# One core, layer 0 and 1 of a diffusion backbone: the body recorded first, then issued in the order of a list schedule of single instructions

## The chip, the cores and the metric

One core of a Trainium2 chip runs the whole program in one launch. The metric is the device time of that launch in microseconds (us); the median over runs is given. Engines are named as in the profile: PE multiplies matrices and PEld loads its weights, DVE, ACT and POOL work on vectors, SP issues nearly all DMAs. Results of PE land in PSUM, which has eight banks, each holding a tile of 128 x 512 fp32.

## What is computed

512 latent tokens and 256 context tokens of width 1024 pass through two layers; the output is the latent stream after a last RMS norm. Layer 0 mixes tokens by windowed attention and by a bidirectional RWKV-7 recurrence, layer 1 by a Fourier transform; each layer then has a squared-ReLU MLP of width 4096. Shift, scale and gate of every norm come from products of a conditioning row with ada_w.

```python
for i in range(DEPTH):
    mod = (s_lat @ ada_w[i] + ada_b[i])[:, None, :]
    sh1, sc1, gt1, sh2, sc2, gt2 = jnp.split(mod, N_MOD, axis=-1)
    h = modulate(rmsnorm(x, norm1_g[i]), sh1, sc1)
    ...
    if even:
        y, yc = hybrid_ab_mixer(h, hc, mix_w_in[j], mix_w_out[j], ...)
    else:
        y = fourier_mixer(h, fourier_w_out[j])
    x = x + gt1 * y
    x = x + gt2 * channel_mlp(modulate(rmsnorm(x, norm2_g[i]), sh2, sc2), mlp_w1[i], mlp_w2[i])
return rmsnorm(x, final_g)
```

The recurrence, per head, token by token, once forward and once backward:

```python
s_kk = jnp.einsum('bhvk,bhk->bhv', S, kk_t)
S = S * w_t[:, :, None, :] - s_kk[..., None] * (kk_t * a_t)[:, :, None, :] + v_t[..., None] * k_t[:, :, None, :]
y_t = jnp.einsum('bhvk,bhk->bhv', S, r_t)
```

## The kernel before

**Precision and weights.** Activations and weights of the dense parts are split into a high and a low half (`fp32r`), and each product is three matmuls: `mm3` (L306 to L308). A weight tile comes by a load of 128 x 512 on SP's queue (`loadh`, L283, from a ring of five buffers `st`), ACT casts its high half (`whi`, L294), DVE subtracts the low half (`wlo`, L295).

**Stages in time.** First adaA (the modulation of the first norm), x and context are loaded, PE turns adaA into shift and scale (`arow`, L441 to L445), and the first three of twenty projection tiles are computed together, latent half (`lat`) then context half (`con`). Tiles 3 to 19 follow (`inproj`): eight `mm3` of 128 x 512 for the latent tokens, eight of 128 x 256 for the context where a tile has one. A tile's end (`post`) shifts it along the tokens (`shifted`, ACT and DVE, L555 to L559), builds keys, values, decay and rates (`key`, `vproj`, `lora` at L633 to L635), and spills them to DRAM (`spill`). From these pages (`page`) each of six blocks of 128 tokens builds its chunk matrices (`prep`, `chunkmats`, `naturals`, `inverse`). The recurrence is a chain over chunks of 64 tokens: `chain_u`, `chain_s`, `chain_y`, where each chunk needs the state of the one before. Attention (`attn0` to `attn2`) runs between them, then the output projection (`outA`, `read`, `outhalf`), MLP 0, the Fourier mixing, MLP 1 and the last norm.

**The other ada products.** 80 columns of adaB (`ada_bg`, L377 to L395) are computed beside the rest: for the first 24, which have two loads each, POOL multiplies (L388) and ACT sums (L389); for the other 56, in MLP 0, DVE does both in one instruction (L391), out of the same ring `st` as the weights.

**What sets the order.** `body` calls the framework directly, inside a Tile context, whose own scheduler places the instructions of each engine. The order of calls in the mixer is a string, PLAN (L1316), in which `:2000` behind a piece is a priority offset; `after(key)` keeps some instructions behind a named one (`tc.issue_after`). Each PSUM tag has banks of its own, three for `mm`, two for `rk`, two for `ch` and one for `iv`, and `phase` names the stage, by which `pst` writes one or two dummy matmuls into a newly taken bank of the attention scores, the reads and the chunk matrices (WARM, L223).

```python
WARM = {('attn1', 'mm'): 1, ('read', 'rk'): 2, ('EB', 'rk'): 1}
PSB = {"mm": 3, "rk": 2, "ch": 2, "iv": 1}
```

Of the kernel before, what the change touches and what calls it, by code (L numbers as in the profile page):

```python
# [5 lines left out]
F32 = mybir.dt.float32  # L6
# [195 lines left out]

def body(tc, I, out):
    nc = tc.nc
# [10 lines left out]
    WARM = {('attn1', 'mm'): 1, ('read', 'rk'): 2, ('EB', 'rk'): 1}  # L215
    PH = [""]
    PSB = {"mm": 3, "rk": 2, "ch": 2, "iv": 1}

    def pst(tag, shape=(128, 512), name="ps"):
        p = ps.tile(list(shape), F32, tag=tag, bufs=PSB[tag], name=name)  # L220
        for _ in range(WARM.get((PH[0], tag), 0)):
            a = p[:]
            pe.matmul(bass.AP(tensor=a.tensor, offset=a.offset, ap=[a.ap[0], [1, 512]]), identr, identr.unsqueeze(1).to_broadcast([128, 4, 128]), start=True, stop=True)  # L223
        return p
# [15 lines left out]
    act.copy(identr, ident)  # L240

# [68 lines left out]
    NI = {}  # L310

    def after(key):
        return tc.issue_after(NI[key].ins) if key else ExitStack()

    def norm_rows(pool_, xs, n, tag, pg="E", pt="E", eng=None, bcast=True):
# [17 lines left out]
        for i in range(nt):  # L333
            for j, a in enumerate(acc):
                NI["p1"] = pe.matmul(p1[:, i : i + 1], a[:, 128 * i : 128 * i + 128], ones1, start=j == 0, stop=j == len(acc) - 1)
# [7 lines left out]
        for i in range(nt):  # L343
            NI["p2"] = pe.matmul(p2[:, 128 * i : 128 * i + 128], rs[:, i : i + 1].to_broadcast([128, 128]), ident, start=True, stop=True)
# [10 lines left out]

    def phase(name):
        PH[0] = name.rstrip("0123456789") if not name.startswith("attn") else name
# [75 lines left out]
    phase("ada0")  # L433
# [100 lines left out]
    def inproj(m, ctx=True):  # L534
        if m < GRP:
            return gl_[m], gctx(m)
        phase(f'proj{m}')
        w = split_w(load(I["win"][m]))
        pl = pst("mm")
        for k in range(8):  # L540
            with after(("lora", m - LT, k) if ("lora", m - LT, k) in NI else None):
                mm3(pl, w, k, hx[k], k == 0, k == 7)
        pc = None
        if ctx:
            pc = pst("ch" if m < 14 else "mm")
            for k in range(8):
                mm3(pc[:, :C], w, k, hc[k], k == 0, k == 7)
        return pl, pc

    def shifted(m, z, pl, pc=None):  # L550
# [3 lines left out]
        for p, off, n in (((pc, 0, C),) if ctx else ()) + ((pl, C if ctx else 0, T),):  # L554
            NI["sh"] = act.activation(z[:, off : off + n], p[:, :n], AF.Identity, scale=mc)  # L555
# [17 lines left out]
    def key(hp, pl, pc):  # L573
        phase(f"key{hp}")
# [27 lines left out]
    def lowrank(pl, pc):  # L602
        phase("lowrank")
# [11 lines left out]
    def lora(hp):  # L615

        phase(f"lora{hp}")
# [9 lines left out]
        for a in range(2):  # L627
            for d in range(2):
                cols = slice(128 * d, 128 * d + 128)
                th = p4((128, TC), "th")  # L630
                for lat, o, n in ((0, 0, C), (1, C, T)):
                    p = pst("rk")
                    pe.matmul(p[:, :n], L_[:, a, cols], x1(a, lat), start=True, stop=False)  # L633
                    NI["lora", hp, 4 * a + 2 * d + lat] = pe.matmul(p[:, :n], hi[:, a, cols], X2[lat], start=False, stop=True)
# [21 lines left out]
    def prep(i, d):  # L656

        phase(f"prep{i}")
# [63 lines left out]
    def chunkmats(i, j):  # L722

        phase(f"EB{i}")
# [31 lines left out]
    def naturals(i, j):  # L756

        phase(f"nat{i}")
# [20 lines left out]
    def inverse(i):  # L779
        phase(f"inv{i}")  # L780
# [116 lines left out]
    def chain_u(i, j):  # L897

        phase(f"chain{i}")
# [29 lines left out]
    def chain_s(i, j):  # L929

        phase(f"chain{i}")
# [16 lines left out]
    def chain_y(i, j):  # L948

        phase(f"chain{i}")  # L950
# [23 lines left out]
    def vproj(hp, pl, pc):  # L974
        phase(f"vproj{hp}")
# [10 lines left out]
    def rproj(hp, pl):  # L986
        phase("rproj")
# [28 lines left out]
    def attk(pl, pc):  # L1016
        phase("attk")
# [7 lines left out]
    def attv(pl, pc):  # L1025
        phase("attv")
# [6 lines left out]
    def attkv():  # L1033

        phase("attkv")
# [31 lines left out]
    def qproj(j, pl):  # L1067
        phase("attq")
# [8 lines left out]
    def gproj(pl):  # L1077
        phase("gate")
# [13 lines left out]
    def attn0(b):  # L1092

        phase("attn1")
# [16 lines left out]
    def attn1(b, kv):  # L1111

        phase("attn1")
# [18 lines left out]
    def attnm(b):  # L1132

        phase("attn1")
# [21 lines left out]
    def attn2(b):  # L1156

        phase("attn2")
# [49 lines left out]
    def bonus(w):  # L1208
        phase("bonus")
# [25 lines left out]
    def outA(ms):  # L1235
        phase("outprojA")
# [12 lines left out]
    def read(w):  # L1249

        phase("read")
# [40 lines left out]
    LT = 2  # L1292
# [14 lines left out]
    def do_ada(n):  # L1307
        with after("sh" if "sh" in NI else None):
            ada_bg(n)
# [7 lines left out]
    tile 0, tile 1, post 0, lora 0, tile 2, post 1, lora 1, tile 3, post 2, lora 2, tile 4, post 3, lora 3, tile 5:300,  # L1317
    ada 2, post 4, prep 0 0:2000, ada 4, prep 0 1, tile 6, post 5, mats 0 0, mats 0 1:2000, nat 0 0:2000, nat 0 1:2000,
    inv 0, tile 7, ada 6, post 6, tile 8, ada 8, post 7, ada 10, tile 9, tile 10, ada 12, post 8:2000, post 9, tile 11,
    ada 14, post 10:500, tile 12, ada 16, post 11, rope, tile 14:200, post 12:1000, prep 1 0:1000, prep 1 1:200,  # L1320
    mats 1 0:200, mats 1 1:200, nat 1 0, nat 1 1:1000, tile 15, post 14, inv 1:300, tile 16, ada 18, post 15,
    prep 2 0:2000, prep 2 1:2000, mats 2 0:2000, mats 2 1:2000, nat 2 0:2000, tile 17, ada 20, post 16, tile 18, ada 22,
    tile 19, post 17, inv 2:1000, post 18:300, ada 24:300, nat 2 1:500, tile 13, post 19, post 13, kv, u 0 0, s 0 0,
    u 0 1, s 0 1, prep 3 0:500, prep 3 1:500, u 1 0:300, s 1 0:300, mats 3 0:500, mats 3 1:1500, nat 3 0:1500,
    nat 3 1:1500, inv 3:1500, qry 0:2000, max 0 0:2000, u 1 1:300, max 0 1:200, row 0:200, s 1 1:300, prep 4 0:1000,
    bonus 2:1000, prep 4 1:1000, mats 4 0:1000, mats 4 1:1000, nat 4 0:1000, nat 4 1:1000, inv 4:1000, ed 2 0,
    ed 2 1:1000, u 2 0, s 2 0, y 2 0, u 2 1, s 2 1, y 2 1, prep 5 0, prep 5 1, mats 5 0, mats 5 1, nat 5 0, inv 5,
    attn 0, bonus 3, ed 3 0, ed 3 1:300, u 3 0, s 3 0:1000, y 3 0:1000, u 3 1:1000, s 3 1:1000, y 3 1:2000, qry 1:200,
    max 1 0:200, max 1 1, row 1:200, u 4 0:100, s 4 0:100, ed 4 0, ed 4 1:100, y 4 0, bonus 4:200, u 4 1, attn 1:1500,
    qry 3:1500, max 3 0:1000, ed 5 1:1500, y 4 1, s 4 1, u 5 0:200, s 5 0:300, ed 5 0, max 3 1:500, row 3:500,  # L1330
    bonus 5:500, y 5 0, u 5 1, y 5 1, attn 3:200, qry 2:500, max 2 0:200, max 2 1:200, row 2:200, attn 2:200, out 0:200,
    out 1, out 2:200, out 3:200, out 4:200, out 5:200, out 6:700, out 7:700, read 4:700, read 5, read 3:300, read 2:300
    """
    for piece in PLAN.replace("\n", " ").split(","):
        what, _, ahead = piece.strip().partition(":")
        what, *args = what.split()
        with tc.high_priority(offset=int(ahead)) if ahead else ExitStack():
            WORK[what](*map(int, args))
    ada_bg(24)
    phase("outproj")  # L1340
# [58 lines left out]
    IA = (None, "p1", "p2")  # L1399
    IB = 2  # L1400

    def mlp(l, xs, ai, sh, gt, nxt):

        phase(f'mlp{l}norm')
# [5 lines left out]
        for f in range(NG):  # L1410
# [7 lines left out]
            with after(IA[f]):  # L1418
                for k in range(8):
                    mm3(p, w, k, us[k], k == 0, k == 7)  # L1420
# [13 lines left out]
        phase(f'mlp{l}')  # L1434
# [92 lines left out]
    phase('fourier')  # L1527
# [7 lines left out]
    for gp in range(2):  # L1535
        for t in range(4):
            p = pst(("mm", "mm", "mm", "ch", "ch", "iv", "mm", "mm")[4 * gp + t], (128, 2, 256))
            with after("p1" if 4 * gp + t >= IB else None):
                for gi in range(2):
                    g = 2 * gp + gi  # L1540
                    for k in range(2):
                        hi, lo = hs[2 * g + k]
                        sl = slice(128 * t, 128 * t + 128)
                        ch, cl = cshi[:, 256 * k : 256 * k + 256], cslo[:, 256 * k : 256 * k + 256]
                        pe.matmul(p[:, gi, :], hi[:, sl], ch, start=k == 0, stop=False)
                        pe.matmul(p[:, gi, :], hi[:, sl], cl, start=False, stop=False)
# [156 lines left out]
```

## Time and profile before

| | |
|---|---|
| runs (us) | 1482.78, 1480.8, 1479.2 |
| median (us) | 1480.8 |
| the profiled execution (us) | 1480.75 |
| its span in the profile (us) | 1479.0 |
| mean granted PE clock | 0.959 |
| dummy matmuls (L223) | 132 |

In the rows below, times are in us from the start of the span. Busy times of a stretch are the time in which an engine worked on an instruction; a PE clock of 1.00 is the full one, and a matmul at a lower clock is counted as busy for longer. PEld overlaps PE. A row of the waits names the waiting instruction, what it waited for, the sum, the number of times and the longest.

### The profile page before, as it was taken

The page shows a single profiled execution, that of the slowest core. Times are in us where ns is not written, and L with a number is a line of the kernel's source. Part 1 is how long each engine was busy: PE and PEld are TensorE (multiplying, and loading weights), DVE is VectorE, ACT ScalarE, POOL GpSimd, SP SyncE. Part 2 cuts the span into 40 slices and gives each one's busy share as a digit, 9 for nine tenths or more (in the row PEclk, how much of TensorE's full clock was granted, in tenths as well). Part 3 has the DMA queues.
Part 4 walks back from the last instruction along what each step waited for, and adds up shares of the span by engine and source line. Part 5 has one row for each costly group of instructions (what it writes and reads, how often), then busy time and mean ns, then how long its engine had stood idle before and what let it go on. Part 6 is the DMA issues. An engine that isn't in the chain of part 4 may idle for free.

```text
span 1479.0 us, 23907 instructions
## 1 busy us (share of the span) xinstructions
PE 1372.7 (93%) x8900; PEld 1084.8 (73%) x8900; DVE 848.5 (57%) x1540; ACT 679.3 (46%) x1331; POOL 327.1 (22%) x352
## 2 busy tenths in 40 slices
PE   6879898988987999898999998999998999999996
PEld 2668777666676667586778876786987888888886
DVE  3544777879876534578555554567697433333334
ACT  3466678474643323444632254433454642255332
POOL 0434676355331432204000000000155000000001
PEclk8879999989988999999999999999999999999998
DMA  9438886565547211224555555556122333333322
GB/s 362 126 117 244 277 251 186 146 200 165 152 125 185 72 54 42 85 65 132 174 178 178 189 170 161 172 192 198 38 72 79 111 96 100 94 100 96 96 93 72
DMA packets 166150, 208.77 MB, mean 141 GB/s; under 512 B 45001, under 2 KB 78793, under 8 KB 166033
## 3 DMA queue, kind: packets, MB, share of 16 engines
q1 hardware_dynamic: 164144, 205.30, 45.1%
q10 hardware_dynamic: 1376, 1.90, 0.4%
q8 instruction: 70, 1.15, 0.3%
q14 instruction: 48, 0.39, 0.1%
q0 software_dynamic: 512, 0.03, 0.0%
HBM read 180.15 MB, written 27.00 MB: 140 GB/s over the span
## 4 chain that ended last, share of the span: by engine, by line
PE 64%; DMA 14%; DVE 12%; ACT 3%; issue 3%; SPq 2%; POOL 1%; DVEq 0%; ACTq 0%; POOLq 0%
PE ps L308 16%; PE ps L307 15%; PE ps L306 15%; DMA st<-adaB_in 6%; DVE wlo L295 3%; PE ps L223 2%; PE ps L1180 2%; PE ps L738 2%; DVE st L391 1%; PE ps L441 1%; DMA D<-Rt 1%; DMA pgk<-spl_k 1%; PE ps L1169 1%; DMA ada<-adaB_in 1%; DMA pgth<-spl_th 1%
## 5 line engine op out<-in xcount | busy, mean ns | idle before, releaser
L294 ACT CAST whi<-st 128x512 fp32r<-128x512 f32 x306 | 188.9, 621 | 395.4 <-PE ps L307 359.4
L295 DVE TENSOR_TENSOR wlo<-st,whi 128x512 fp32r<-128x512 f32 x306 | 226.0, 742 | 168.6 <-ACT whi L294 167.0
L308 PE MATMUL ps<-hhi,wlo 128*128 128x512 f32 x600 | 240.7, 401 | 15.8 <-DVE wlo L295 15.6
L306 PE MATMUL ps<-hhi,whi 128*128 128x512 f32 x600 | 238.7, 399 | 3.7 <-ACT hhi L353 3.0
L307 PE MATMUL ps<-hlo,whi 128*128 128x512 f32 x600 | 237.7, 397 | 0.6 <-DVE hlo L354 0.5
L308 PE MATMUL ps<-zhi,wlo 128*128 128x512 f32 (+1 forms) x528 | 203.0, 385 | 5.3 <-DVE wlo L295 5.3
L306 PE MATMUL ps<-zhi,whi 128*128 128x512 f32 (+1 forms) x528 | 202.4, 384 | 0.0
L307 PE MATMUL ps<-zlo,whi 128*128 128x512 f32 (+1 forms) x528 | 202.1, 383 | 0.0
L308 PEld LDWEIGHTS ps<-hhi,wlo 128*128 128x128 f32 x600 | 114.6, 191 | 48.3 <-DVE wlo L295 24.8
L306 PEld LDWEIGHTS ps<-hhi,whi 128*128 128x128 f32 x600 | 114.7, 191 | 29.0 <-ACT hhi L353 3.8
L307 PEld LDWEIGHTS ps<-hlo,whi 128*128 128x128 f32 x600 | 114.7, 191 | 25.5 <-DVE hlo L354 1.8
L308 PEld LDWEIGHTS ps<-zhi,wlo 128*128 128x128 f32 x528 | 99.1, 188 | 27.8 <-DVE wlo L295 8.6
L391 DVE CUSTOM_DVE_ANT_0 st<-st,sB,vec 128x512 f32<-128x512 f32 x56 | 42.2, 754 | 127.8 <-DMA st<-adaB_in 127.6
L307 PEld LDWEIGHTS ps<-zlo,whi 128*128 128x128 f32 x528 | 99.2, 188 | 19.5
L306 PEld LDWEIGHTS ps<-zhi,whi 128*128 128x128 f32 x528 | 99.2, 188 | 19.1
L1512 POOL TENSOR_TENSOR wa<-st 128x512 f32<-128x512 f32 x8 | 11.9, 1493 | 358.2 <-DMA st<-fw_in 342.3
L388 POOL TENSOR_TENSOR ada<-ada,sB 128x512 f32<-128x512 f32 x48 | 71.0, 1507 | 44.1 <-DMA ada<-adaB_in 27.5
L1660 POOL TENSOR_TENSOR rs<-ms,pw 128x2 f32<-128x2 f32 x2 | 1.4, 704 | 333.6 <-DVE ms L1658 333.6
L223 PE MATMUL ps<-identr 128*128 128x512 f32 x132 | 59.5, 475 | 7.2 <-ACT Vn L1062 2.2
L1454 DVE TENSOR_TENSOR zlo<-s,zhi 128x512 fp32r<-128x512 f32 x64 | 44.0, 688 | 31.2 <-ACT zhi L1453 31.2
L738 PEld LDWEIGHTS ps<-pr,gq 64*128 64x128 f32 x384 | 43.9, 193 | 12.2 <-issue 8.9
L738 PE MATMUL ps<-pr,gq 64*128 64x128 f32 (+1 forms) x384 | 50.7, 289 | 2.2 <-DVE gq L712 2.1
(451 smaller groups left out, 2644.1 us busy)
## 6 DMA issues: line engine op xcount, KB each, us to landing
st<-w_in SPq DMA_DIRECT2D x256, 256.0 KB, 2.8
st<-adaB_in SPq DMA_DIRECT2D x112, 256.0 KB, 3.4
ada<-adaB_in SPq DMA_DIRECT2D x48, 256.0 KB, 5.1
st<-win_in SPq DMA_DIRECT2D x40, 256.0 KB, 4.0
spl_th<-th SPq DMA_DIRECT2D x16, 384.0 KB, 2.8
pgth<-spl_th SPq DMA_DIRECT2D x24, 256.0 KB, 5.1
st<-adaA_in SPq DMA_DIRECT2D x16, 256.0 KB, 5.4
st<-adaA_in SPq DMA_DIRECT2D x8, 512.0 KB, 7.5
```

What stands on the lines that cost most here:

```text
L223: pe.matmul(bass.AP(tensor=a.tensor, offset=a.offset, ap=[a.ap[0], [1, 512]]), identr, identr.unsqueeze(1).to_broadcast([128, 4, 128]), st ...
L294: act.copy(hi, st)
L295: dve.tensor_tensor(lo, st, hi, ALU.subtract)
L306: pe.matmul(o, whi, x[0], start=first, stop=False)
L307: pe.matmul(o, whi, x[1], start=False, stop=False)
L308: pe.matmul(o, wlo, x[0], start=False, stop=last)
L388: pool.tensor_tensor(st, st, su, ALU.mult)
L391: dve.tensor_tensor_reduce(st, st, su, 1.0, col if u else V(vec, "adb", i), ALU.mult, ALU.add, col)
L441: pe.matmul(pa[q : q + 32, :], sT[:, k, :], mats[k], start=k < 4, stop=k >= 4)
L738: pe.matmul(p[:, hp, :wd], o.GQ[d][c][rows, hp, :], o.PR[d][c][rows, hp, :wd], start=True, stop=True)
L1180: pe.matmul(po[64 * kv : 64 * kv + 64, :], Vn[0][:, kt // 128, 64 * kv : 64 * kv + 64], pts[kv], start=(i == 0), stop=(i == len(keyt) - 1))
L1454: dve.tensor_tensor(lo, s, hi, ALU.subtract)
```

## The change

`body` is given a `Plan` in place of the Tile context. Each call on an engine is recorded with what it reads and writes (`Rec`, `Queue`, `VPool`), and nothing is issued. `solve` then takes the recorded instructions with an assumed cost each (`cost`), ranks each by the longest way from it to the end, and goes through time: whenever an engine is free, it starts the ready instruction of the highest rank, on PE with a preference for the matmul shape of the last one (STICK, MODE). It follows a model of PE's clock and, where PE would stand still (`fill`), puts a dummy matmul into a free bank if the model asks for it. The eight PSUM banks are shared: a tile takes any free bank (`claim`), as long as some are left for the other tags (BANKS). `issue` gives the instructions to the framework in that order, each tied to the one before it on its engine. PLAN keeps the order of its pieces and loses the offsets; `phase`, `after` and the WARM table go. Every instruction of the new kernel is issued from L656, and every dummy from L646. Both kernels have the same instructions on DVE (1542), ACT (1291), POOL (357) and SP (862); PE has 6955 and 6920, the difference being 132 dummies and 97. 66 of PE's instructions wait for another of PE's in the kernel before, 174 in the changed one.

```diff
+class Plan:
+    WAIT = {"tensor": 54, "vector": 33, "scalar": 32, "gpsimd": 60, "sync": 60}
+    WIN, COLD, WARM = 3413.3, 0.27, 0.66
+    MODE, STICK = 100, 1500
+    KEEP, RAISE, SPARE = 0.7, 0.9, 100
+    RING = {"mm": 3, "rk": 2, "ch": 2, "iv": 1}
+    BANKS = {"mm": 2, "rk": 1, "ch": 2, "iv": 1}
...
+    def cost(self, r):
...
+        if r.op == "dma_start":
+            return 430.0, 2900.0
...
+    def solve(self):
...
+        for k in range(n - 1, -1, -1):
+            b = 0.0
+            for q in succ[k] + slot[k]:
+                same = recs[q].eng == recs[k].eng == "tensor"
+                b = max(b, rank[q] + (cost[k][0] if same else cost[k][1] + W[recs[q].eng]))
+            rank[k] = max(b, cost[k][1])
+        key = [-(rank[k] + recs[k].lead) for k in range(n)]
...
+        def fill(a, t):
+            nonlocal lastmode
+            while banks and banks[0][0] + 100 < a:
+                c = clock(a)
+                w, f = int(a // self.WIN), 0.93
+                d = 227 / c + (self.MODE if lastmode != (128, 128) else 0)
+                if a + d > t - self.SPARE or act.get(w, 0.0) > (self.KEEP if c == 1 else self.RAISE) * self.WIN:
+                    break
...
+        def claim(k):
...
+                    others = sum(max(v - held.get(x, 0), 0) for x, v in self.BANKS.items() if x != g[1])
+                    if len(banks) < c + others:
+                        return False
...
+            if r.op == "dma_start":
...
+                srv = max(srv, t + 1400) + nb / row / 16 * (19 + 0.0346 * row)
+                end[k] = srv + 750
...
+    def issue(self, tc):
+        seq = self.solve()
...
+            if isinstance(k, tuple):
+                p, i = pools["ps"].tile([128, 512], F32, tag=f"bank{k[0]}", bufs=1, name="warm"), real[self.warm.tensor.name][:]
+                i = tc.nc.tensor.matmul(p, i, i.unsqueeze(1).to_broadcast([128, 4, 128]), start=True, stop=True)
...
+            i = getattr(getattr(tc.nc, r.eng), r.op)(*[tr(a) for a in r.args], **{x: tr(a) for x, a in r.kw.items()})
+            if r.eng in last:
+                tc.add_manual_dep(i.ins, last[r.eng], need, reason="order")
...
 def body(tc, I, out):
-    nc = tc.nc
+    nc = tc
...
     def pst(tag, shape=(128, 512), name="ps"):
-        p = ps.tile(list(shape), F32, tag=tag, bufs=PSB[tag], name=name)
-        for _ in range(WARM.get((PH[0], tag), 0)):
...
+        return ps.tile(list(shape), F32, tag=tag, name=name)
...
-    ada 2, post 4, prep 0 0:2000, ada 4, prep 0 1, tile 6, post 5, mats 0 0, mats 0 1:2000, nat 0 0:2000, nat 0 1:2000,
+    ada 2, post 4, prep 0 0, ada 4, prep 0 1, tile 6, post 5, mats 0 0, mats 0 1, nat 0 0, nat 0 1,
...
+    plan = Plan(nc)
+    body(plan, I, out)
     with tile.TileContext(nc, schedule_with_timeline_sim=True) as tc:
-        body(tc, I, out)
+        plan.issue(tc)
```

The order on an engine is shown at three places. The first is the start. On PE, the kernel before runs the end of the first three tiles (weights `gh` and `gl`), and then the context half of tile 3 (weights `whi` and `wlo` with the context's `hchi` and `hclo`):

```order
L308 MATMUL ps<-hchi,gl 128x256
L306 MATMUL ps<-hchi,gh 128x256
L307 MATMUL ps<-hclo,gh 128x256
L308 MATMUL ps<-hchi,gl 128x256
L306 MATMUL ps<-hchi,whi 128x256
L307 MATMUL ps<-hclo,whi 128x256
L308 MATMUL ps<-hchi,wlo 128x256
L306 MATMUL ps<-hchi,whi 128x256
```

Its latent half (with `hhi` and `hlo`) comes some sixty rows later, among the low-rank products of `lora` (L633, L634):

```order
L593 MATMUL ps<-cst,nr 64x128 x12
L633 MATMUL ps<-X1c,LW_767 128x256
L634 MATMUL ps<-X2c,LH_770 128x256
L306 MATMUL ps<-hhi,whi 128x512
L307 MATMUL ps<-hlo,whi 128x512
L308 MATMUL ps<-hhi,wlo 128x512
L633 MATMUL ps<-X1l_628,LW_767 128x512
L634 MATMUL ps<-X2l,LH_770 128x512
```

The changed kernel's PE at the end of the same three tiles:

```order
L656 MATMUL ps<-hchi,gl 128x256
L656 MATMUL ps<-hchi,gh 128x256
L656 MATMUL ps<-hclo,gh 128x256
L656 MATMUL ps<-hchi,gl 128x256
L656 MATMUL ps<-hhi,whi 128x512
L656 MATMUL ps<-hlo,whi 128x512
L656 MATMUL ps<-hhi,wlo 128x512
L656 MATMUL ps<-hhi,whi 128x512
```

The latent half of tile 3 now stands directly behind them. On SP, at the same place of the program, the kernel before issues the first projection weights (`win`) between the first sixteen and the last eight loads of adaA:

```order
L426 DMA st_152<-adaA_in 128x512
L426 DMA st_154<-adaA_in 128x512
L283 DMA st<-win_in 128x512 x5
L466 DMA st_266<-adaA_in 128x1024
L466 DMA st_268<-adaA_in 128x1024
L466 DMA st_270<-adaA_in 128x1024
```

In the changed kernel all loads of adaA stand ahead of them, and x ahead of adaA:

```order
L656 DMA st_235<-adaA_in 128x1024
L656 DMA c_238<-cT_in 128x256
L656 DMA st_242<-adaA_in 128x1024
L656 DMA st_245<-adaA_in 128x1024
L656 DMA st<-win_in 128x512 x5
L656 DMA sB<-crow_in 128x1024
```

The second place is on PE among the attention scores of a query block (`kst`, `qst` and `k_`, `q_`) and the state chain (`zs`, `ab`); L223 is a dummy. Before:

```order
L1125 MATMUL ps<-k_3167,q_3756 128x256
L923 MATMUL ps<-zs,ab 64x64 x16
L223 MATMUL ps<-identr 128x512
L1126 MATMUL ps<-kst,qst 128x256
L1127 MATMUL ps<-k_3167,q_3756 128x256
L223 MATMUL ps<-identr 128x512
L1124 MATMUL ps<-kst,qst 128x256
L1125 MATMUL ps<-k_3167,q_3756 128x256
L223 MATMUL ps<-identr 128x512
```

And in the changed kernel, where `cst,gq` are the transposed operands (`naturals`) of another block:

```order
L656 MATMUL ps<-zs,ab 64x64 x2
L656 MATMUL ps<-k_2917,q_3061 128x256
L656 MATMUL ps<-cst,gq 128x128 x2
L656 MATMUL ps<-kst,qst 128x256
L656 MATMUL ps<-cst,gq 128x128
L656 MATMUL ps<-k_2917,q_3061 128x256
L656 MATMUL ps<-kst,qst 128x256
L656 MATMUL ps<-cst,gq 128x128
L656 MATMUL ps<-k_2917,q_3061 128x256
L656 MATMUL ps<-cst,gq 128x128 x4
```

The dummies between the scores are gone, and other blocks' matmuls stand there. The third place is on DVE in MLP 0, where the ada products (ISA, two rows each) alternate with the weight splits. Before:

```order
L295 TENSOR_TENSOR wlo<-st,whi 128x512
L391 ISA st,adv<-st,sB,vec 128x512
L391 ISA adv 128x1
L295 TENSOR_TENSOR wlo<-st,whi 128x512
L391 ISA st,adv<-st,sB,adv 128x512
L391 ISA adv 128x1
L295 TENSOR_TENSOR wlo<-st,whi 128x512
L391 ISA st,adv<-st,sB,vec 128x512
L391 ISA adv 128x1
```

In the changed kernel:

```order
L656 TENSOR_TENSOR wlo<-st,whi 128x512
L656 ISA st,adv<-st,sB,adv 128x512
L656 ISA adv 128x1
L656 TENSOR_TENSOR wlo<-st,whi 128x512
L656 ISA st,adv<-st,sB,vec 128x512
L656 ISA adv 128x1
L656 SCALAR_TENSOR_TENSOR xn<-ps,adv,xo 128x512
L656 TENSOR_TENSOR wlo<-st,whi 128x512
L656 ISA st,adv<-st,sB,adv 128x512
L656 ISA adv 128x1
```

The two kinds still take turns there; a gate of the residual stream (`xn`) stands among them.

More of the change, by code (lines that the diff above doesn't have):

```diff
@@ L540, in inproj @@
         for k in range(8):
-            with after(("lora", m - LT, k) if ("lora", m - LT, k) in NI else None):
-                mm3(pl, w, k, hx[k], k == 0, k == 7)
+            mm3(pl, w, k, hx[k], k == 0, k == 7)
         pc = None
@@ L1417, in mlp @@
             p = pst("ch" if f < 2 else "iv")
-            with after(IA[f]):
-                for k in range(8):
-                    mm3(p, w, k, us[k], k == 0, k == 7)
+            for k in range(8):
+                mm3(p, w, k, us[k], k == 0, k == 7)
             pool.tensor_tensor(pr[0], pr[0], pr[1], ALU.add)
```

491 lines of the change are left out of this document (406 added, 85 removed).

## The prediction

> **What bounds the kernel now.** I read the page first, then the busy times by stage, then the instructions in order of time where a stage begins, then the waits. The page:
>
> ```profile
> span 1479.0 us, 23907 instructions
> PE 1372.7 (93%) x8900; PEld 1084.8 (73%) x8900; DVE 848.5 (57%) x1540; ACT 679.3 (46%) x1331; POOL 327.1 (22%) x352
> ```
>
> PE looks full, but its 93% hides half-clock time, dummy matmuls and stretches in which it does little. So I cut the span where the work changes: loads, the first three projection tiles, the other tiles, the state chain in two parts, the output projection, MLP 0, Fourier mixing, MLP 1, the end.
>
> ```profile
> core 0: us, PE busy (x) PEld busy (x) DVE busy (x) ACT busy (x) POOL busy (x), PEclk, DMA share, GB/s
> 0.00:34.00 34.00, 21.43 (x73) 8.41 (x74) 10.64 (x29) 12.32 (x21) 1.52 (x6) 0.85 0.98 362
> 34.00:104.00 70.00, 57.69 (x295) 43.36 (x294) 37.44 (x63) 39.80 (x81) 29.31 (x31) 0.80 0.39 123
> 104.00:285.00 181.00, 166.72 (x1040) 134.94 (x1040) 122.66 (x186) 121.81 (x287) 105.63 (x100) 0.97 0.75 229
> 285.00:460.00 175.00, 157.29 (x2079) 120.36 (x2078) 145.88 (x293) 96.14 (x207) 67.54 (x99) 0.92 0.55 158
> 460.00:617.00 157.00, 144.80 (x1588) 97.97 (x1587) 72.17 (x184) 53.77 (x119) 50.45 (x51) 0.92 0.28 76
> 617.00:662.00 45.00, 45.00 (x200) 37.28 (x199) 33.82 (x55) 20.93 (x35) 0.00 (x0) 1.00 0.25 77
> 662.00:1046.00 384.00, 365.81 (x1583) 293.62 (x1582) 221.19 (x439) 151.49 (x255) 21.07 (x18) 0.99 0.54 169
> 1046.00:1140.00 94.00, 86.57 (x559) 75.73 (x558) 79.46 (x111) 46.84 (x101) 44.77 (x39) 0.98 0.21 67
> 1140.00:1460.00 320.00, 320.00 (x1443) 266.12 (x1442) 117.72 (x173) 135.06 (x225) 0.00 (x0) 1.00 0.31 94
> 1460.00:1479.00 19.00, 7.42 (x57) 6.96 (x55) 7.56 (x13) 1.16 (x3) 6.81 (x8) 0.73 0.33 111
> ```
>
> From 617 on PE is the bound: 825 us of its 862 are busy, in MLP 1 all of 320 at clock 1.00. No order of the same matmuls shortens that much. The first 617 us are different: no engine is full, the clock is 0.80 to 0.97, and part of PE's busy time there is dummies. The same stages for the dummies' line alone (us, PE busy, PEld busy, clock, DMA share, GB/s):
>
> ```profile
> 104.00:285.00 181.00, 8.99 (x20) 4.01 (x20) 0.97 0.75 229
> 285.00:460.00 175.00, 30.22 (x66) 12.54 (x66) 0.92 0.55 158
> 460.00:617.00 157.00, 20.30 (x48) 8.25 (x46) 0.92 0.28 76
> ```
>
> **The change part by part.** The work itself is the same; only order, PSUM banks and dummies differ. So the sum is over PE time that holds no useful matmul, stage by stage, and how much of it the other engines let go.
>
> *The start, 0 to 104.* The recorded order loads all sixteen rows of adaA ahead of the first projection weights. By the sizes in the code 12.5 MB (x 2, context 1, adaA 8.4, constants 0.8 and vec 0.1, in binary units) plus two weight pieces come first; at the 362 GB/s of the first row that is 36 us, with cast and subtraction some 38, against 34 before: 4 us lost. What is won lies behind the third tile:
>
> ```profile
> 76.54 0.28 PE L308 MATMUL ps<-hchi,gl 128*128 128x256 f32 x1
> 81.94 0.55 PE L306 MATMUL ps<-hchi,whi 128*128 128x256 f32 x1 [5.13 <-DVE k L557]
> ...
> 103.84 0.28 PE L634 MATMUL ps<-X2c,LH 128*128 128x256 f32 x1
> 103.95 0.40 PE L306 MATMUL ps<-hhi,whi 128*128 128x512 f32 x1
> 104.19 0.40 PE L307 MATMUL ps<-hlo,whi 128*128 128x512 f32 x1
> ```
>
> PE waits 5.13 us for a fixed bank that DVE's shift must empty, then takes tile 3's context half, and comes to its latent half only at 103.95. With eight shared banks two are free when the first three tiles hold six, and the order puts tile 3's latent matmuls straight behind. Of the 70 us of this stage 57.69 are busy, so 12.3 us are idle, and at clock 0.80 up to a fifth of the busy time, some 12 to 14 us, is slowness that dense matmuls would remove. Together 26 us; less the 4 lost, and since ACT (39.8) and DVE (37.4) must do the same shifts, I take 16. Bounds: 0 and 26 gained.
>
> *The other tiles, 104 to 285.* Idle 14.3 us and dummies 9.0: 23 us at most. ACT and DVE stand at 122 of 181, POOL at 106, so none forbids it, but DMA is at 0.75. I take 10, somewhat under the half. Bounds 0 and 23.
>
> *The chain, 285 to 617.* Idle is 17.7 and 12.2, dummies are 30.2 and 20.3. In the first part DVE is busy 145.9 of 175, so it can shrink by 29 us at most before DVE is the bound; in the second DVE and ACT are under half, and idle and dummies are 32.5. The order keeps 24 dummies where 114 stood. But u, s and y of each step wait for each other, so some idle time only changes place: I take half of both, 14 + 16 = 30. Bounds 0 and 61.
>
> *The dense part, 617 to 1479.* Idle is 18.2 in MLP 0 and 7.4 around the Fourier stage. In MLP 0 it is DVE that waits, and PE behind it:
>
> ```profile
> DVE st L391 <- DMA st<-adaB_in: 133.2, 60, 4.8
> PEld ps L308 <- DVE wlo L295: 34.4, 35, 2.7
> PE ps L308 <- DVE wlo L295: 20.8, 24, 2.3
> ```
>
> On DVE the new order still alternates one ada product with one or two weight splits, over the same ring of five buffers, so this stall mostly stays. I take 4; bounds 0 and 18.
>
> *Added waits.* PE's instructions that wait for PE itself rise from 66 to 174, since a dummy or a new group may take a bank that PE wrote last. Behind such a matmul stands all of PE's queue. The matmul at 103.95 lasts 0.40 and the next starts 0.24 after it, so waiting for its end costs 0.16: 108 such waits are 17 us. Most are dummies in idle time, where they hide; if the idle time isn't there, they cost in full. I take 4; bounds 0 and 17.
>
> Sum, against the profiled execution's 1480.75 us (span 1479.0; the median of the runs is 1480.8, so no correction): 16 + 10 + 30 + 4 - 4 = 56, or **1424.75 us, about 1425**.
>
> **The rivals.**
>
> *A, the gaps close.* If the greedy order packs as well as the busy sums allow, the bounds hold rather than the halves: 26 + 23 + 61 + 6 = 116, or 1365 us. For it: in 460 to 617 no engine but PE is over half busy. Against: the chain's steps are serial, and no stage before 617 has packed so well.
>
> *B, the clock falls.* The dummies were there to keep the clock up, and three quarters of those in the chain go. Where PE idles, the clock is low, and the next stretch is full:
>
> ```profile
> 460.00:480.00 20.00, 11.93 (x261) 10.29 (x261) 9.31 (x24) 7.21 (x17) 3.13 (x5) 0.74 0.73 182
> 480.00:500.00 20.00, 20.00 (x196) 9.71 (x192) 14.76 (x15) 11.33 (x19) 14.78 (x14) 1.00 0.19 57
> ```
>
> If the chain ran at the 0.80 of stage 34 to 104 instead of 0.92, its 251.6 us of PE work (302.1 busy less 50.5 dummies) would become 289: 38 us back, 1463. For it: 90 fewer dummies there. Against: the planner follows the clock itself and keeps dummies for it. [...]
>
> *C, slower: late loads in a fixed order.* In its ranks the planner counts 2.9 us for a load; the trace has, by load (KB each, median us to landing):
>
> ```profile
> ada<-adaB_in SPq DMA_DIRECT2D x48, 256.0 KB, 5.1
> pgth<-spl_th SPq DMA_DIRECT2D x24, 256.0 KB, 5.1
> ```
>
> and by wait (us in total, times, longest):
>
> ```profile
> POOL ada L388 <- DMA ada<-adaB_in: 27.5, 7, 13.8
> ACT ada L389 <- POOL ada L388: 7.6, 9, 1.5
> ```
>
> Each of the 48 ada pieces passes through POOL and then ACT, between the casts that feed PE. If every one came 5.1 - 2.9 = 2.2 us later than its place assumes and ACT stood still for it, 106 us are lost: 1425 + 106 = 1531. It decides against the change once over half of that (56 us) lies on the path. For it: an engine's queue is in order, so one late load holds every cast behind it, and the denser tile stage asks more of DMA, which is at 0.75. Against: before, too, the order was fixed when the kernel was built, and only 27.5 and 7.6 us were waited.
>
> *D, nothing gained.* The serial chain sets the end of the mixer, and what PE wins in the tiles it waits for later: 1480.75, within 0.2%.
>
> **How the numbers follow.** Forecast 0.48, A 0.18, B 0.12, C 0.16, D 0.06. 0.2% of 1480.8, 3 us, is about what a measurement of this kernel can tell from no change. Forecast, A and B are all faster by more: 0.78. D is 0.06, C 0.16. The range goes from 1355, ten below A, to 1490, which takes in B, D and a forecast with no term but the added waits at half; C's 0.16 and some 0.04 below stay out.
>
> **What would show it.** Tile 3's latent half should start near 66 us on PE with no wait for a bank; the first chain matmul should come before 285; dummies after that should be few, with clock at 0.9 or above; PE should start the output projection near 565; MLP 0 should still show DVE waiting for adaB by about 100 us or more. ACT or DVE waiting long for ada or paged loads below 300 us would speak for C, clock rows under 0.85 in the chain for B. The forecast is wrong if the mixer's end does not move, or if the dense part grows because a late loader stalls the splits.

## The result and the profile after

The changed kernel takes 1431.19 us in the median of four runs (1429.67 to 1433.22), the kernel before beside it 1481.79. The ratio, for which one run before of 1498.1 counts too, is 0.9637 (95% interval 0.9566 to 0.9708): 3.6% faster. The forecast was 1425.

The head of the profile of the changed kernel, then its stretches, cut where the program begins the same work as at the cuts of before (PE, PEld, DVE, ACT, POOL busy with their instructions, PE's clock, DMA share, GB/s):

```profile
span 1427.9 us, 23855 instructions
PE 1337.8 (94%) x8865; PEld 1083.8 (76%) x8865; DVE 850.9 (60%) x1540; ACT 671.9 (47%) x1331; POOL 328.8 (23%) x352
```

```profile
0.00:38.00 38.00, 23.75 (x107) 9.23 (x107) 13.08 (x31) 14.08 (x28) 7.40 (x14) 1.00 0.98 360
38.00:69.00 31.00, 28.76 (x168) 24.68 (x167) 28.44 (x45) 25.06 (x51) 14.41 (x16) 1.00 0.48 154
69.00:297.00 228.00, 199.08 (x1261) 163.75 (x1259) 157.92 (x246) 158.34 (x363) 128.38 (x135) 0.91 0.75 224
297.00:545.00 248.00, 223.98 (x3196) 179.19 (x3195) 166.38 (x376) 106.99 (x222) 87.18 (x116) 0.81 0.42 117
545.00:617.00 72.00, 71.31 (x437) 55.05 (x433) 45.79 (x100) 34.54 (x78) 13.51 (x10) 0.98 0.34 99
617.00:984.00 367.00, 364.42 (x1591) 295.68 (x1590) 233.45 (x449) 152.07 (x260) 21.45 (x18) 1.00 0.56 177
984.00:1080.00 96.00, 87.02 (x591) 77.90 (x590) 77.44 (x105) 45.09 (x99) 49.63 (x39) 1.00 0.21 64
1080.00:1414.00 334.00, 333.72 (x1500) 273.84 (x1499) 121.34 (x181) 134.55 (x232) 0.71 (x1) 1.00 0.28 90
1414.00:1428.00 14.00, 5.77 (x33) 4.51 (x32) 7.02 (x12) 1.16 (x3) 6.12 (x7) 0.83 0.45 150
```

The same view of the kernel before, for the three stretches that answer to 297:545, 545:617 and 617:984:

```profile
285.00:557.00 272.00, 246.20 (x3307) 181.58 (x3307) 189.76 (x390) 126.28 (x263) 99.00 (x134) 0.92 0.47 132
557.00:657.00 100.00, 95.88 (x540) 69.90 (x537) 58.44 (x137) 42.07 (x91) 18.99 (x16) 0.96 0.24 71
657.00:1043.00 386.00, 367.81 (x1582) 294.87 (x1581) 223.38 (x443) 152.74 (x257) 21.07 (x18) 0.99 0.54 168
```

Read against each other: the state chain takes 248 us for 272, at a **lower** clock (0.81 for 0.92); what follows it up to MLP 0 takes 72 for 100; MLP 0 takes 367 for 386. The table gives the start of some PE rows in both traces (us). The chain is counted here and below from its first `chain_u` matmul (`vu,ab`) to its last (`zs,ab`); the last `chain_y` matmul comes later in both, at 568.0 before, among the last block's attention, and at 549.3 in the changed kernel.

| PE row | before | changed | difference |
|---|---|---|---|
| first matmul of the first three tiles | 33.7 | 38.3 | +4.6 |
| last of these tiles | 76.5 | 68.7 | -7.8 |
| first latent matmul of tile 3 | 104.0 | 68.9 | -35.1 |
| last latent matmul of a tile | 293.2 | 275.9 | -17.4 |
| first `chain_u` matmul | 284.8 | 297.3 | +12.5 |
| last `chain_u` matmul | 557.5 | 544.9 | -12.6 |
| first matmul of MLP 0 | 657.3 | 617.2 | -40.1 |
| last matmul of MLP 0 on z | 1043.3 | 984.1 | -59.2 |
| last matmul of MLP 1 on z | 1465.0 | 1414.4 | -50.5 |
| end of the last matmul | 1471.0 | 1420.0 | -51.0 |

So 40 us came from the mixer and 19 from MLP 0, and some 8 were given back between MLP 0 and the end. The chain did not begin earlier: it began 12.5 us later and was 25 us shorter, and the stretch behind it was 27.5 us shorter.

### The profile page after: what moved, and what is told of

It reads as the page before. It is cut to its first block, busy times and chain, and to the rows that moved or that the text cites. A ratio compares the mean times of both kernels' runs of the same rounds, so it can differ in the third digit from the quotient of the medians.

```text
span 1427.9 us, 23855 instructions
## 1 busy us (share of the span) xinstructions
PE 1337.8 (94%) x8865; PEld 1083.8 (76%) x8865; DVE 850.9 (60%) x1540; ACT 671.9 (47%) x1331; POOL 328.8 (23%) x352
## 4 chain that ended last, share of the span: by engine, by line
PE 57%; DVE 3%; DMA 1%; issue 1%; ACT 0%; POOL 0%; DVEq 0%; ACTq 0%
PE ps L656 57%; DVE ht L656 1%; DVE wlo L656 1%; DVE fwlo L656 0%; DVE hlo L656 0%; DVE x L656 0%; DMA st<-adaB_in 0%; DMA q<-ml 0%; PE warm L646 0%; DVE wb L656 0%; DVE ulo L656 0%; DVE o L656 0%; DMA st<-wout_in 0%; DVE y L656 0%; DVE sq L656 0%
## 5 line engine op out<-in xcount | busy, mean ns | idle before, releaser
L656 ACT CAST whi<-st 128x512 fp32r<-128x512 f32 x306 | 187.7, 619 | 409.6 <-PE ps L656 370.7
L656 DVE TENSOR_TENSOR wlo<-st,whi 128x512 fp32r<-128x512 f32 x306 | 226.1, 749 | 221.8 <-ACT whi L656 159.8
L656 PE MATMUL ps<-hlo,whi 128*128 128x512 f32 x600 | 230.5, 394 | 4.1 <-DVE hlo L656 4.1
L656 PE MATMUL ps<-hhi,whi 128*128 128x512 f32 x600 | 232.0, 397 | 2.2 <-ACT hhi L656 1.7
L656 PE MATMUL ps<-hhi,wlo 128*128 128x512 f32 x600 | 228.4, 394 | 5.1 <-DVE wlo L656 5.0
L656 PE MATMUL ps<-zhi,whi 128*128 128x512 f32 (+1 forms) x528 | 203.1, 389 | 0.6 <-ACT whi L656 0.6
L656 PE MATMUL ps<-zlo,whi 128*128 128x512 f32 (+1 forms) x528 | 202.2, 389 | 0.0
L656 PE MATMUL ps<-zhi,wlo 128*128 128x512 f32 (+1 forms) x528 | 199.3, 389 | 0.3 <-DVE wlo L656 0.3
L656 PEld LDWEIGHTS ps<-hhi,wlo 128*128 128x128 f32 x600 | 113.0, 189 | 30.4 <-DVE wlo L656 7.0
L656 PEld LDWEIGHTS ps<-hlo,whi 128*128 128x128 f32 x600 | 113.2, 189 | 29.0 <-DVE hlo L656 5.7
L656 PEld LDWEIGHTS ps<-hhi,whi 128*128 128x128 f32 x600 | 112.7, 188 | 27.3 <-ACT hhi L656 2.5
L656 PEld LDWEIGHTS ps<-zhi,whi 128*128 128x128 f32 x528 | 98.8, 188 | 24.0 <-ACT whi L656 1.6
L656 PEld LDWEIGHTS ps<-zhi,wlo 128*128 128x128 f32 x528 | 98.8, 188 | 23.3 <-DVE wlo L656 0.9
L656 PEld LDWEIGHTS ps<-zlo,whi 128*128 128x128 f32 x528 | 98.6, 188 | 22.3
L656 POOL TENSOR_TENSOR rs<-ms,pw 128x4 f32<-128x4 f32 (+1 forms) x7 | 6.2, 885 | 407.4 <-DVE ms L656 407.4
L656 POOL TENSOR_TENSOR wa<-st 128x512 f32<-128x512 f32 x8 | 13.0, 1629 | 342.2 <-DMA st<-fw_in 325.5
L656 POOL TENSOR_TENSOR ada<-ada,sB 128x512 f32<-128x512 f32 x48 | 66.2, 1399 | 42.2 <-DMA ada<-adaB_in 28.6
L656 DVE CUSTOM_DVE_ANT_0 st<-st,sB,vec 128x512 f32<-128x512 f32 x56 | 42.0, 750 | 44.1 <-DMA st<-adaB_in 44.1
L656 PE MATMUL ps<-pr,gq 64*128 64x128 f32 (+1 forms) x384 | 50.0, 341 | 14.7 <-DVE gq L656 11.8
L656 PEld LDWEIGHTS ps<-pr,gq 64*128 64x128 f32 x384 | 44.2, 240 | 20.7 <-issue 13.3
L656 DVE TENSOR_TENSOR zlo<-s,zhi 128x512 fp32r<-128x512 f32 x64 | 44.2, 691 | 25.7 <-ACT zhi L656 25.4
L656 DVE CUSTOM_DVE_ANT_0 st<-st,sB,adv 128x512 f32<-128x512 f32 x56 | 41.9, 749 | 14.2 <-DMA st<-adaB_in 13.6
```

Of the source, the lines that this page charges most:

```text
L656: i = getattr(getattr(tc.nc, r.eng), r.op)(*[tr(a) for a in r.args], **{x: tr(a) for x, a in r.kw.items()})
```

## The experiments

Each was timed in five rounds beside the kernel before; the ratio is to that kernel's runs on the same chip. Where an expectation speaks of "the z tiles", these are the squared activations `zhi` and `zlo`, the moving operands of the second product of each MLP. In the rows of PE a small matmul (64 columns here) stands as two rows (the changed kernel's page counts 8865 rows of PE for its 6920 instructions), so rows are counted, and not matmuls, where it says so.

**What MLP 1 gave back.** In MLP 1 PE is busy throughout at clock 1.00 in both traces, and yet it is slower afterwards. Rows of PE in the changed kernel, the first and the last of 25 (start, duration):

```profile
1199.63 0.40 PE L656 MATMUL ps<-zlo,whi 128*128 128x512 f32 x1
...
1205.23 0.40 PE L656 MATMUL ps<-zlo,whi 128*128 128x512 f32 x1
```

24 steps in 5.60 us: one every 0.233. In the kernel before it is one every 0.227. The matmuls on `hhi` and `hlo` kept 0.227 in both. The addresses in the compiled programs give a suspect: in the kernel before, pool `Q` begins with a tile `zpad` of 8 floats that nothing uses, and the z tiles begin at 32 modulo 64 bytes. A recorded tile that nothing uses is never claimed, so in the changed kernel they begin at 0 modulo 64.

Run a_pad8, the changed kernel with that tile back:

```diff
                 pools[name], ends[name] = cm.__enter__(), cm
+                if name == "Q":
+                    pools[name].tile([128, 8], F32, name="zpad")
```

> The changed kernel with an unused tile of 8 floats (32 bytes a partition) in front of pool Q again, so that the z tiles of both MLPs begin 32 bytes later, as in the kernel before. Theory P (the place of z in memory): the 1584 matmuls on z start 0.227 us apart as before and not 0.233, 1584 x 0.0065 = 10 us less, about 1421. Rival O (PE alternates between two output tiles there, or loads interfere): the pace stays 0.233 and the time 1431.

Run b_nopad, the kernel before without it:

```diff
-    Q.tile([128, 8], F32, name="zpad")
```

> The kernel before without the line that puts 8 unused floats in front of pool Q: its z tiles begin 32 bytes earlier, at the same place modulo 64 bytes as in the changed kernel. Theory P: z matmuls 0.233 us apart and not 0.227, 10 us more, about 1492. Rival O: no change, 1482, pace 0.227.

Rows of PE of a_pad8, 24 steps apart, and then of b_nopad, also 24:

```profile
1199.76 0.39 PE L658 MATMUL ps<-zhi,wlo 128*128 128x512 f32 x1
...
1205.20 0.39 PE L658 MATMUL ps<-zhi,wlo 128*128 128x512 f32 x1
```

```profile
1205.94 0.40 PE L308 MATMUL ps<-zhi,wlo 128*128 128x512 f32 x1
...
1211.54 0.40 PE L308 MATMUL ps<-zhi,wlo 128*128 128x512 f32 x1
```

5.44 us with the 32 bytes, 5.60 without, in either kernel: the pace goes with the place. b_nopad took 1489.63 (1.0069, 1.0032 to 1.0106): 5 to 16 us more, which takes in the 10 expected and can't tell them from less. a_pad8 took 1428.44 (0.9646, 0.9606 to 0.9686), no measurable difference from the changed kernel. By stretches, from the first latent matmul of MLP 1 to its last on z, the changed kernel takes 345.0 us and a_pad8 340.5 (before 340.8, b_nopad 345.3), while in MLP 0, which also waits for its weights (PE idles 18.2 us there before, 2.6 in the changed kernel), only some 1.5 us come back in a_pad8 and b_nopad loses nothing there; and the mixer of a_pad8, with the same order, was 4.4 us slower than in the changed kernel's profile, which one profile of each can't tell from scatter. So theory P holds for the pace and for 4.5 us in MLP 1, in both directions.

**Were the dummies in the way?** Up to MLP 0 PE's dummies fell from 59.5 us to 19.1 by the rows of their lines, 40 us, which is just what the mixer won. Two runs take all dummies out. b_nowarm is the kernel before:

```diff
-    WARM = {('attn1', 'mm'): 1, ('read', 'rk'): 2, ('EB', 'rk'): 1}
+    WARM = {}
```

> The kernel before without any of its 132 dummy matmuls, nothing else changed in its source. Theory D (the mixer's 40 us came from dummies that stood in the way): 40 of their 59.5 us come back, 1435 to 1445. Rival C (they hold the clock): the chain falls to 0.8 or less and the time is 1482 or more. Rival N (the order is what won): within 1475 to 1485.

and a_nofill the changed one:

```diff
         def fill(a, t):
+            return
             nonlocal lastmode
```

> The changed kernel with its planner putting in no dummy at all (97 fewer). Theory D: they stood in idle time and hold little, 1426 to 1436. Rival C (even these few hold the clock): more stretches at half clock before 617 us and at the norms, 1445 to 1470.

b_nowarm took 1482.15 (1.0016, 0.9979 to 1.0053): no difference, so theory D falls. C's 1482 or more is met to the letter, but there is no loss clear of the noise. Its chain, in the view of stretches:

```profile
292.00:564.00 272.00, 242.25 (x3181) 184.14 (x3183) 186.77 (x395) 123.17 (x251) 98.00 (x134) 0.81 0.47 129
```

The clock fell from 0.92 to 0.81, about as C wanted, and the stretch is as long as before to the microsecond. That is a net figure: 39 us of dummy rows fell out of this stretch, and PE's other rows were busy for 242.2 us where they had been for 222.9. Whether dummies and clock are both worth nothing here, or the one pays for the other, the run doesn't tell. a_nofill took 1433.92 (0.9678, 0.9638 to 0.9717), which the changed kernel's interval takes in. So in either kernel all dummies together are worth nothing that was measured, and that the two 40s agree was chance.

**What of the planner wins the mixer?** a_fixbanks divides the banks again:

```diff
-                    others = sum(max(v - held.get(x, 0), 0) for x, v in self.BANKS.items() if x != g[1])
-                    if len(banks) < c + others:
+                    if mine + c > self.RING[g[1]]:
```

> The changed kernel with its PSUM banks divided among the tags again (3, 2, 2 and 1, by a limit of how many each tag may hold). Theory S (shared banks let the fourth projection tile start behind the third and so win the first 300 us): the last latent tile ends 10 to 17 us later and the time is 1440 to 1448. Rival Q (the order wins it, banks are no limit): 1427 to 1437.

It took 1434.67 (0.9667, 0.9623 to 0.9711). The fourth tile's latent half starts at 72.4 us in place of 68.9, the mixer ends at 617.0 as before that edit. Q holds: the medians differ by 3.5 us, and the intervals overlap.

a_written keeps the banks, the clock model and the list, but takes what was written first:

```diff
-    MODE, STICK = 100, 1500
+    MODE, STICK = 100, 30
...
-        key = [-(rank[k] + recs[k].lead) for k in range(n)]
+        key = [float(k) for k in range(n)]
```

(STICK is in units of the key, so here it reaches over 30 instructions of the written order, and the preference for the last shape is not quite the same.)

> The changed kernel with its planner taking the ready instruction that was written first in the body (with the pieces in the order of the string) in place of the one with the longest way to the end; banks, dummies and clock model as they are. Theory R (the rank by the longest way wins the mixer): most of its 40 us come back, 1455 to 1475. Rival M (starting whatever is ready, in the written order, does it): 1430 to 1445.

It took 1468.68 (0.9881, 0.9840 to 0.9923). MLP 0 begins at 662.3 us: all 40 us of the mixer are gone, and MLP 0 itself still takes 372. R holds. The loss lies mostly behind the chain: the chain begins at 296.5, as in the changed kernel, and is 9 us longer, but from its end to MLP 0 it is 109 us where the changed kernel has 72.

a_stick0 takes away only the preference for the last matmul's shape:

```diff
-    MODE, STICK = 100, 1500
+    MODE, STICK = 100, 0
```

> The changed kernel with its planner not preferring a matmul of the same shape as the last one on PE (STICK 0); all else as it is. Theory G (PE loses time when neighbouring matmuls differ in their rows and columns): the chain from 297 to 545 us grows by 30 us or more, 1460 to 1500. Rival H (such changes cost nothing on the chip): 1425 to 1440.

It took 1601.08 (1.0754, 1.0703 to 1.0805), slower than the kernel before and by far more than theory G asked for. Its chain runs from 299 to 704. PE rows from it (start, time from the first start to the last end of the group, active rows x columns, count):

```profile
520.68 1.54 PE L656 MATMUL ps<-edl,vu 128*64 128x64 f32 x22
522.01 0.42 PE L656 MATMUL ps<-vu,gq 128*64 128x64 f32 x2
...
527.01 0.47 PE L656 MATMUL ps<-vu,gq 128*64 128x64 f32 x2
527.41 0.47 PE L656 MATMUL ps<-pr,St 64*64 64x64 f32 x2
527.81 0.47 PE L656 MATMUL ps<-vu,gq 128*64 128x64 f32 x2
528.22 0.47 PE L656 MATMUL ps<-pr,St 64*64 64x64 f32 x2
528.62 0.47 PE L656 MATMUL ps<-vu,gq 128*64 128x64 f32 x2
```

22 rows of one shape, eleven matmuls, take 1.33 us to the next start, 0.12 for each matmul. Where one matmul of 128*64 and one of 64*64 take turns, each takes 0.40: 0.28 more for each change, here at half clock: in the changed kernel's chain a small matmul in a series takes mostly 0.11 at a granted clock of 0.50 and 0.06 at 1.00, and 0.40 and 0.41 in the two places where one stands between others at 0.50. Over the whole chain of this run, the next start after a 64*64 row that another shape follows comes in one of two clusters, 0.148 or 0.242 us later (220 gaps); in the trace the granted clock is 1.00 at the first and 0.50 at the second, and in the changed kernel's chain such gaps are 0.148 or 0.149 at 1.00 (21 of 24) and 0.240 to 0.243 at 0.50 (all 13). Where its own shape follows it is mostly 0.007 and then 0.05 at full clock, 0.007 and then 0.10 at half, but the second row behind a change comes 0.11 and 0.16 later, and both gaps together make the price. G holds, and this was in no step of the prediction.

Counting the changes of active rows x columns between neighbouring PE rows of the chain, and its length:

| kernel | changes of shape | chain, us | clock |
|---|---|---|---|
| a_stick0 | 685 | 405.1 | 0.67 |
| b_ring6 (below) | 287 | 318.5 | 0.78 |
| before | 262 | 272.7 | 0.92 |
| b_nowarm | 243 | 272.6 | 0.81 |
| a_written | 204 | 256.8 | 0.81 |
| a_padwarm (below) | 186 | 246.7 | 0.84 |
| a_fixbanks | 185 | 247.4 | 0.84 |
| changed | 180 | 247.6 | 0.81 |
| a_nofill | 169 | 241.8 | 0.84 |
| a_padstick (below) | 142 | 237.4 | 0.85 |

From 685 to 180 it is 157 us for 505 changes, 0.31 each; from 180 to 142, 10.2 us for 38, 0.27 each. The clock doesn't order this table: at 0.84, a_fixbanks and a_padwarm are as long as the changed kernel at 0.81. At 0.3 us, the 82 changes between before and the changed kernel are 25 us, as much as the chain gained. That they are its cause is argued from the price, not shown, for among the kernels that the framework's scheduler ordered the price doesn't fit: b_nowarm is no shorter than before with 19 changes fewer, b_ring6 is 46 us longer with 25 more.

a_attnlate holds back the last query block's attention:

```diff
-        WORK[what](*map(int, args))
+        with tc.lead(-100000 if what in ('qry', 'max', 'row', 'attn') and args[0] == '2' else 0):
+            WORK[what](*map(int, args))
```

> The changed kernel with the attention of query block 2, the last one, taken only when nothing else is ready (its rank lowered by 100 us). Theory T (moving this attention out of the tail into the chain's gaps wins 25 us): the time from the last chain matmul to the first matmul of MLP 0 grows from 72 to 90 or more and the total is 1450 to 1460. Rival U (the chain gets shorter by as much once the attention is out of it): 1428 to 1436.

It took 1451.47 (0.9777, 0.9730 to 0.9823). From the last chain matmul to MLP 0:

```profile
538.00:631.00 93.00, 90.45 (x520) 66.86 (x521) 53.31 (x124) 38.29 (x86) 18.79 (x16) 1.00 0.26 76
```

93 us where the changed kernel has 72 and before had 100, and the chain is 7 us shorter in return. T holds: this attention in the chain's gaps is worth 14 us net at the start of MLP 0, and 20 at the end.

**What shortened MLP 0?** PE idled 18.2 us there before, now 2.6. Waits of PE before, and of DVE in the changed kernel, both in MLP 0 alone (us in total, times, longest):

```profile
PE ps L308 <- DVE wlo L295: 15.5, 20, 2.3
```

```profile
DVE st L656 <- DMA st<-adaB_in: 57.7, 56, 3.6
DVE wlo L656 <- ACT whi L656: 44.3, 44, 3.2
```

DVE's waits for adaB fell from 133.2 to 57.7, and splits that DVE makes late hardly stop PE any more (0.3 us, once, for 15.5). The ring that ada and weights share was tried first, as b_ring6:

```diff
-SGB, STB = 10, 5
+SGB, STB = 10, 6
```

> The kernel before with six buffers of the weight ring st in place of five (STB 6). Theory B (MLP 0 was held by the round of this ring, free, issue, landing, use, which the ada products and the weights share): from the first matmul of MLP 0 to its last it takes 370 to 375 us and not 386, the whole 1466 to 1473. Rival V (DVE's order holds it, a split behind a waiting ada product, whatever the ring): 386 and 1480 to 1486.

It took 1525.58 (1.0283, 1.0237 to 1.0330). MLP 0 takes 380.4 us for 386, and PE idles 18.1 there as before: B falls for all but 5 us. MLP 0 begins 50 us later: the mixer's chain grows from 273 to 319 us. Its order is another one, which the framework's scheduler chose with the sixth buffer; why it is so much longer stays open (287 changes of shape against 262 don't pay for it).

Then, as a_serial, PE was bound to the written order in MLP 0 only:

```diff
+        if eng == "tensor":
+            if self.serial:
+                pre.add(self.prev)
+            self.prev = r.n
         self.recs.append(r)
...
+        tc.serial = l == 0
         for half in range(2):
...
+        tc.serial = False
         return xs
```

> The changed kernel with its planner bound, in MLP 0 alone, to issue PE's matmuls in the written order, one output tile after the other, as the kernel before does; the order of the other engines is planned as before. Theory I (MLP 0 got 19 us shorter because PE now works on two output tiles by turns and has other matmuls at hand while a split is late): PE idles 10 to 18 us there in place of 2.6, from its first matmul to the last of MLP 0 it takes 377 to 386 us and not 367, the whole is 1441 to 1450. Rival V (DVE's and SP's order did it): idle under 5, 365 to 370, 1428 to 1436.

It took 1442.19 (0.9734, 0.9693 to 0.9776), of which MLP 0 accounts for 5:

```profile
623.00:995.00 372.00, 367.30 (x1594) 296.72 (x1593) 226.06 (x446) 154.84 (x259) 21.92 (x18) 1.00 0.54 174
```

```profile
DVE st L661 <- DMA st<-adaB_in: 109.5, 52, 3.9
```

The total lies where theory I put it, but not by I's way: 372 us and 4.7 us idle, though DVE waits for adaB nearly as long as before. So I falls for the most part: PE's taking turns is worth 5 of the 19 us. The other 14 should lie in what the two planned kernels share and the one before has not, the order on DVE, ACT and SP: of the 122 low halves that meet `hhi` or `zhi` there, 26 were ready less than 0.15 us ahead of their first matmul in the kernel before, 11 in a_serial, 2 in the changed kernel. That order wasn't tried alone, so its part is argued, not shown. The other 6 us of this run were lost ahead of MLP 0, which began at 623.0 with a mixer of the same kind of order, as in a_pad8.

**Two versions that might be better.** Both also have the 32 bytes of a_pad8. a_padwarm lets dummies push the plan a little:

```diff
-                if a + d > t - self.SPARE or act.get(w, 0.0) > (self.KEEP if c == 1 else self.RAISE) * self.WIN:
+                if a + d > t - (-300 if c == 1 else -400) or act.get(w, 0.0) > (self.KEEP if c == 1 else self.RAISE) * self.WIN:
```

> The changed kernel with the 32 bytes in front of pool Q and with a planner that may let a dummy run up to 0.3 us (0.4 at half clock) into the next planned matmul. Theory K (the half clock from 273 to 380 us costs): clock rows of 0.8 and more there, 10 to 15 us less than the 1428 with the 32 bytes alone, 1413 to 1418. Rival L (the chain waits for DVE and for its own steps there): the clock rises, the time stays within 1424 to 1434.

It took 1434.61 (0.9674, 0.9625 to 0.9723). The clock from 280 to 380 rose only from 0.62 in a_pad8 to 0.69, far from the 0.8 asked for, so the run doesn't tell K from L; it isn't faster. What it shows is the price of dummies that push: in the first 46 us they stand between adaA's products with 9.1 us in 26 rows, 3.2 in 7 in a_pad8, and the first three tiles begin at 44.9 for 38.1, 6.8 us later, which is about what the run lost. a_padstick changes one number more than a_pad8:

```diff
-    MODE, STICK = 100, 1500
+    MODE, STICK = 100, 5000
```

> The changed kernel with the 32 bytes in front of pool Q and with a planner that keeps to the last matmul shape more firmly (STICK 5000 for 1500), which leaves some 223 changes of shape on PE where 273 stood. Theory G (each change costs PE 0.15 us at full and 0.24 at half clock): 50 x 0.15 to 0.24 = 8 to 12 less than 1428, 1416 to 1420. Rival W (what is gained is lost by leaving the order of rank): 1426 or more.

It took 1418.61 (0.9565, 0.9518 to 0.9612), the fastest of all kernels here: 9.8 us under a_pad8, where 8 to 12 were forecast from the price of a change. The two intervals just touch, but the chain, 10.3 us shorter than in a_pad8, says where it lies.

## Why the prediction came out right, step by step

The total was 6 us off, with terms that were partly wrong and made up for each other: ahead of MLP 0 the sum had 52 us (16, 10 and 30, less 4 for waits) and 40 came, behind that it had 4 and 11 came. That the total fits so well is luck; that the mixer's order holds most of the gain was foreseen, the way it does so was not.

- **Late start (4 us lost)**: right, 4.6.
- **Start (16 gained) and tiles (10)**: the step that fell is that this time would go straight into an earlier chain. Tile 3 moved as forecast, 35 us ahead, the last tile ended 17.4 us earlier where 26 were forecast, but the chain began 12.5 us later, with the chain's preparation behind the tile work: the inverse's first matmul stands at 277.7, behind the last tile's 275.9, where before it stood at 265.8, ahead of 293.2. The reason given, shared banks, was wrong as well: a_fixbanks has fixed shares and the same start within 4 us. (A fifth of 57.69 is 11.5 and not 12 to 14, so the upper bound was 24; nothing hangs on it.)
- **Chain (30 gained)**: too small and for the wrong reason. Up to MLP 0 it was 25 in the chain and 27.5 behind it. The prediction let it come out of idle time and dummies; b_nowarm shows that taking dummies out gives nothing net. What gave it was the planner's rank and its preference for a shape (a_written, a_stick0): behind the chain the last attention, which now stands in the chain's gaps, is worth 14 (a_attnlate); in the chain fewer changes of matmul shape would pay for all of it (82 x 0.3), as far as the price carries over. The page before had no row on a change of shape, but its trace had the pairs of neighbouring rows, and STICK and MODE stood in the diff.
- **Dense part (4 gained)**: mis-sized. "This stall mostly stays" was wrong: MLP 0 won 19, and the idle time there, the prediction's own bound of 18.2, fell by 15.6; the rest of the program lost 8, of which 4.5 are the z tiles' place and some 4 in the Fourier stage stay open.
- **Added waits (4 lost)**: not seen. No row of the changed kernel's waits shows PE waiting for PE, and of its 172 rows that wait for a semaphore of PE's own, 166 start before the row ahead of them has ended.
- **Rival B, the clock**: the clock fell and the time didn't rise. The chain's clock came to 0.81, by the rows above, which was priced at 38 us; b_nowarm shows the same fall in the old order at no net price. There the dummies' own time went too, so what a lower clock costs by itself stays open.
- **Rival C, late loads**: not seen. POOL waits for adaB as long as before (27.5 us):

```profile
POOL ada L656 <- DMA ada<-adaB_in: 28.6, 10, 5.5
```

- **Rivals A and D**: the gaps of MLP 0 closed, for which A's sum took only 6 of the bound of 18, those of the mixer did not: by the gaps between PE's rows it idles 69.1 us up to MLP 0 before and 70.1 now. D's step came true in part: what PE won in the tiles it didn't bring to the chain.
- **The signs named**: tile 3's latent half came at 68.9 (66 forecast) and the output projection at 565.6 (565), though that hit means less than it seems, since before it began at 611.8 and ran in one piece, and now it runs among the reads and takes 6 us longer; the chain's start, the clock of 0.9 and DVE's 100 us for adaB did not come.

## What to carry to other kernels

Before a stretch of small matmuls is called serial or short of clock, count the neighbours on PE whose active rows x columns differ: here each change cost the chain about 0.3 us, as much as two to three small matmuls of 0.12 us, and without the one number that keeps like with like the whole kernel was 12% slower (1601 for 1431). Idle time and dummies in a stretch are not its reserve until a run without them is shorter: here the chain took 272.7 us with 39 us of dummies and 272.6 without. After any change in how tiles are allocated, compare the pace of the same matmul before and after in a stretch where PE is full; an unused tile may have been doing work (here 0.227 us a matmul with it and 0.233 without).

## What was not expected of the hardware

Matmuls of 128x512 on the same values, in the same order, start 0.227 us apart where the moving tile begins at 32 modulo 64 bytes and 0.233 where it begins at 0, in two kernels each; whether its place against the weights' (at 32 in all four) matters wasn't tried. The chain at clock 0.81 without dummies (b_nowarm, 272.6 us) was as long as at 0.92 with 39 us of them (before, 272.7). In a_stick0, after a row of a small 64*64 matmul the next of another shape started 0.148 us later at a granted clock of 1.00 and 0.242 at 0.50; a small matmul between two of another shape held PE for 0.40 us at half clock, one in a series of its own shape for 0.12.
